# Three copies per block of transposed q and k: VectorE's queue or GpSimd's

## The chip, the cores and the metric

The kernel runs on one core of a Trainium2 chip. A core has five engines that run side by side, each with its own in-order queue of instructions: TensorE (PE, matrix products, with PEld for its weight loads), VectorE (DVE), ScalarE (ACT), GpSimd (POOL) and SyncE (SP, which here does nothing but start DMA transfers). An instruction that has to wait for another engine holds up everything behind it in its own queue. The metric is the device time of one execution in microseconds, as the median of several runs; less is better.

## The reference

One decoder layer over 2048 positions of width 1024. A single projection of the normalised input feeds three token mixers; each is gated, and one output projection adds the result to the input.

```python
def hybrid_layer(x, norm_g, w_in, b_f, q_norm_g, k_norm_g, w_pool, pool_scale, w_out):
    h = rms_norm(x, norm_g)
    proj = jnp.einsum('bsd,de->bse', h, w_in)
    (fq, fk, fv, fg, ff, px, pg, sq, sk, sv, sg) = jnp.split(proj, idx, axis=-1)
    fq = rms_norm(to_heads(fq, FOX_HEADS), q_norm_g)
    fk = rms_norm(to_heads(fk, FOX_HEADS), k_norm_g)
    log_f = jax.nn.log_sigmoid(ff + b_f).transpose(0, 2, 1)
    fox_out = from_heads(forgetting_attention(fq, fk, to_heads(fv, FOX_HEADS), log_f)) * jax.nn.silu(fg)
    pool_out = multiscale_pool(px, w_pool, pool_scale) * jax.nn.silu(pg)
    sb = stick_breaking_attention(to_heads(sq, SB_HEADS), to_heads(sk, SB_HEADS), to_heads(sv, SB_HEADS))
    sb_out = from_heads(sb) * jax.nn.silu(sg)
    mixed = jnp.concatenate([fox_out, pool_out, sb_out], axis=-1)
    return x + jnp.einsum('bse,ed->bsd', mixed, w_out)
```

Forgetting attention ("Fox", 8 heads of 64) is causal softmax attention with a bias from cumulated forget gates. Stick-breaking attention ("Stick", 4 heads of 64) weights position s by sigmoid(z) times the product of one minus sigmoid over the positions between s and t. The pooling branch takes trailing means over 2 to 16 positions.

## The kernel before

The sequence is stored backwards and cut into 16 blocks of 128 positions. The work runs in overlapping stages: Fox over its first four heads (names end in `a`), Fox over the other four (`b`), Stick over its four heads (`s`) with the pooling branch mixed in (`p`), and the output projection (`pr`, `mt`, `xr`). Within a stage the loop runs over blocks, in each block over four heads. Numbers are kept as pairs of float16 (a high and a low part), so most products are made twice or three times.

For each block of `a`, `b` and `s` the function `stacks` (line 454) does the following. ScalarE and VectorE write q and k as float16 pairs into `st` (lines 340 and 341). One DMA transpose, started by SP, turns `st` into `qT`: its first four of eight slots hold k of the four heads, the other four hold q; high parts are in partitions 0 to 63, low parts in 64 to 127. A little later in program order (`later(SCD, ...)`) `place` runs three copies:

```python
        def place():
            pick(KCE, 0).tensor_copy(Kc[j // 4][:, :, o_:o_ + P], qT[:, 0:NH])
            for k in range(2):
                pick(SWE, k).tensor_copy(qT[k * HD:k * HD + HD, 0:NH], qT[HD - k * HD:P - k * HD, NH:2 * NH])
            placed.add(tag)
```

The first (line 466) puts k into the key cache `Ka`, `Kb` or `Ks`, 128 partitions of 512 elements. The other two (line 468) overwrite the place of k in `qT` with q whose high and low halves have changed places, 64 partitions of 512 elements each. `pick` chooses the engine: `v` is VectorE, `g` GpSimd. The products of the scores (line 403, into `spa`, `spb`, `sps`) read both the cache and `qT`, so the first scores of a block wait for all three copies.

What else stands in the queues that matter here. VectorE: in Fox the biased maximum of the scores (`L`, `mm`, line 735), in Stick the running product of the sigmoids (`rrs`, a scan, line 882), in all three the low part of the weights (`pp`, line 432), and the small vectors of the norms and the gates. GpSimd: in Fox the gain on q (`qn`, line 717), the scaling of the block's output (`om`, line 758) and the start of the transfer of the cumulated gates (`cd`, line 562); in Stick a small set to one value (line 877), the causal mask of the sigmoids (a select, line 876, without which the scan can't start) and the copy of the scan's last column (`left`, line 886); at the end the product with the gate (`mt`, line 1033). The weights go through a DMA transpose (`tt<-pp`, line 434) to the product with v (lines 445 and 446, in Stick 902 to 904).

The order in every queue is set before the run by a planner that walks the program and places instructions by its own estimates of time. It is not written out by hand, so a change of one instruction's engine moves others too.

Of the kernel before, what the change touches and what calls it, by code (L numbers as in the profile page):

```python
# [36 lines left out]
GR4 = 0  # L37
GR2 = 1
QSB = 2
SWE = 'vv'  # L40
KCE = 'v'
SCD = 5
M5 = 2
FE = 's'
# [80 lines left out]
def hybrid(ctx: ExitStack, tc, xN, w_in, w_pT, w_out, ng, b_f, qg, kg, w_pool, p_scale, bands, out):  # L125
# [19 lines left out]
    def pick(pattern, k):  # L145
        return {"v": v, "g": g, "s": s}[pattern[k % len(pattern)]]
# [307 lines left out]
    def stacks(tag, j, qsrc, ksrc, sc, Kc):  # L454
# [10 lines left out]
# [5 lines that stand above are left out]
# [842 lines left out]
```

## Time and profile before

| What | Value |
|---|---|
| Median of 3 runs | 1407.43 us (1404.51 to 1409.54) |
| The profiled execution, its own time | 1408.75 us |
| Its span from first to last instruction | 1407.0 us |
| Mean granted TensorE clock | 0.941 of full speed |
| PE busy | 1199.0 us, 85% |
| DVE busy | 1036.6 us, 74% |
| ACT busy | 752.8 us, 54% |
| POOL busy | 182.1 us, 13% |
| DMA queue of SP, share of 16 engines | 80.7% |

Busy time is summed per engine over the span. An engine with a low share can still be the one for which others wait at a given place; the share says only how much room it has on average. The profiled execution is 1.3 us above the median.

### The profile page before, as it was taken

What the parts mean: (1) busy time and instruction counts of PE and PEld (TensorE: products, weight loads), DVE (VectorE), ACT (ScalarE), POOL (GpSimd) and SP (SyncE); (2) the same over time, 40 slices, a digit from 0 to 9 for tenths busy, and PEclk for the clock granted to TensorE, in tenths of its full rate; (3) what the DMA queues carried; (4) which work ended last, traced back from release to release, by engine and by line L of the source; (5) the groups of instructions that cost most, each with busy time, mean ns of one, the idle gap of its engine ahead of it and who ended that gap; (6) DMA issues with size and microseconds to landing.
All of it is one profiled execution on the core that took longest, in us unless ns stands there. A gap on an engine that the chain in (4) does not pass through costs nothing.

```text
span 1407.0 us, 24844 instructions
## 1 busy us (share of the span) xinstructions
PE 1199.0 (85%) x9068; PEld 637.2 (45%) x9068; DVE 1036.6 (74%) x2309; ACT 752.8 (54%) x1430; POOL 182.1 (13%) x327
## 2 busy tenths in 40 slices
PE   7788878786867898989887889889898898889998
PEld 3344444353434454545444444445454454444443
DVE  5787788687967567788788867768687789864741
ACT  6565666665745457556676845455454655431210
POOL 0111010000000001000101022212111113222400
PEclk9899999898989899999999989989999999999999
DMA  6789999999999989988899989786887779999863
GB/s 216 180 186 199 213 220 187 194 217 181 252 180 178 219 210 219 189 171 157 170 219 183 194 199 205 166 178 145 173 169 167 161 178 261 234 253 314 219 178 91
DMA packets 617066, 275.24 MB, mean 196 GB/s; under 512 B 552560, under 2 KB 590832, under 8 KB 616944
## 3 DMA queue, kind: packets, MB, share of 16 engines
q1 hardware_dynamic: 605600, 239.93, 80.7%
q10 hardware_dynamic: 10832, 33.67, 7.6%
q8 instruction: 71, 1.16, 0.3%
q14 instruction: 51, 0.42, 0.1%
q0 software_dynamic: 512, 0.07, 0.0%
HBM read 102.60 MB, written 34.67 MB: 98 GB/s over the span
## 4 chain that ended last, share of the span: by engine, by line
PE 40%; DMA 25%; DVE 15%; issue 9%; ACT 8%; POOL 2%; SPq 1%; ACTq 0%; DVEq 0%; POOLq 0%
PE pr L318 10%; DMA tta<-ppa 6%; DVE rrs L882 5%; DMA ttb<-ppb 5%; PE pqkb L318 4%; PE pvgb L318 4%; DMA xTx<-ppx 3%; PE pqks L318 3%; DMA qTa<-sta 3%; PE pp L318 2%; PE spb L403 2%; PE pqka L318 2%; PE pvgs L318 2%; DMA xTm<-ppm 2%; PE ob L445 2%
## 5 line engine op out<-in xcount | busy, mean ns | idle before, releaser
L318 PE MATMUL pr<-wo,xTm 128*128 128x512 f16 x768 | 171.6, 385 | 6.5 <-DMA xTm<-ppm 5.1
L429 ACT CAST pps<-rrs 128x640 f16<-128x640 f32 (+7 forms) x96 | 76.3, 796 | 129.5 <-DVE rrs L882 113.8
L882 DVE TENSOR_TENSOR_SCAN rrs<-rrs 128x640 f32<-128x640 f32 (+7 forms) x64 | 106.4, 1663 | 27.2 <-POOL rrs L876 18.9
L318 PEld LDWEIGHTS <-xTm 128*128 128x128 f16 x768 | 75.5, 99 | 99.0 <-issue 6.3
L745 ACT ACTIVATE Lb<-Lb,nmb 128x640 f32<-128x640 f32 (+7 forms) x96 | 85.5, 892 | 62.4 <-DVE nmb L739 59.4
L318 PEld LDWEIGHTS <-xTs 128*128 128x128 f16 x768 | 75.1, 100 | 91.3 <-issue 11.5
L318 PEld LDWEIGHTS <-xTb 128*128 128x128 f16 x768 | 75.1, 102 | 89.7 <-issue 15.2
L745 ACT ACTIVATE La<-La,nma 128x640 f32<-128x640 f32 (+7 forms) x96 | 85.4, 890 | 48.7 <-DVE nma L739 42.5
L318 PEld LDWEIGHTS <-xTx 128*128 128x128 f16 x720 | 69.8, 101 | 83.2 <-issue 13.9
L432 DVE TENSOR_TENSOR pps<-rrs,pps 128x640 f16<-128x640 f32 (+7 forms) x96 | 87.3, 919 | 17.0 <-ACT pps L429 15.6
L318 PE MATMUL pp<-auxp,xTp 128*128 128x512 f16 x384 | 96.7, 404 | 2.6 <-DVE vo L341 2.6
L318 PE MATMUL pvgb<-wb,xTb 128*128 128x512 f16 x384 | 97.4, 395 | 1.2 <-DVE omb L779 1.0
L318 PE MATMUL pqkb<-wb,xTb 128*128 128x512 f16 x384 | 97.0, 399 | 1.6 <-DVE oma L779 1.3
L432 DVE TENSOR_TENSOR ppb<-Lb,ppb 128x640 f16<-128x640 f32 (+7 forms) x96 | 88.9, 936 | 11.3 <-ACT ppb L429 10.8
L318 PE MATMUL pqks<-ws,xTs 128*128 128x512 f16 x384 | 95.6, 394 | 0.2 <-DVE vo L341 0.2
L403 PE MATMUL spa<-Ka,qTa 128*128 128x512 f16 (+3 forms) x320 | 79.6, 363 | 18.5 <-DVE mma L735 16.0
L318 PE MATMUL pvgs<-ws,xTs 128*128 128x512 f16 x384 | 92.7, 384 | 1.9 <-DVE ym L1004 1.9
L432 DVE TENSOR_TENSOR ppa<-La,ppa 128x640 f16<-128x640 f32 (+7 forms) x96 | 88.2, 934 | 7.0 <-ACT ppa L429 6.7
L445 PE MATMUL oa<-Va,tta 128*128 128x128 f16 x544 | 61.9, 227 | 36.3 <-DMA tta<-ppa 35.0
L445 PE MATMUL ob<-Vb,ttb 128*128 128x128 f16 x544 | 63.3, 226 | 32.7 <-DMA ttb<-ppb 31.5
L318 PE MATMUL pqka<-wa,xTx 128*128 128x512 f16 x336 | 87.7, 407 | 1.5 <-DVE nma L739 1.5
L874 ACT ACTIVATE rrs<-sps,nc 128x640 f32<-128x640 f32 (+7 forms) x96 | 80.1, 863 | 15.7 <-PE sps L403 15.2
(306 smaller groups left out, 2709.0 us busy)
## 6 DMA issues: line engine op xcount, KB each, us to landing
xn<-in_xN_dram SPq DMA_DIRECT2D x16, 512.0 KB, 6.2
xTd<-xTx ACTq DMA_DIRECT2D x16, 512.0 KB, 4.1
xTb<-xTd ACTq DMA_DIRECT2D x16, 512.0 KB, 4.5
xTs<-xTd ACTq DMA_DIRECT2D x16, 512.0 KB, 4.4
xTp<-xTd ACTq DMA_DIRECT2D x16, 512.0 KB, 4.3
go<-gat SPq DMA_DIRECT2D x16, 512.0 KB, 7.1
mt<-mix SPq DMA_DIRECT2D x16, 512.0 KB, 5.5
xr<-in_xN_dram SPq DMA_DIRECT2D x16, 512.0 KB, 4.1
```

The source lines that it names most:

```text
L318: t.matmul(psum, x[:, xa, kt, :], wt[:, wa, c0:c0 + n], start=(kt == 0 and i == 0), stop=(kt == KT - 1 and i == 2))
L403: t.matmul(sp[:, b - c0 + off:e - c0 + off], qT[:, a * NH + h, :], Kc[b // 512][:, h, b % 512:b % 512 + e - b], start=(a == 0), stop=(a == ...
L429: s.copy(hi, p32)
L432: lo_eng.tensor_tensor(lo, p32, hi, ALU.subtract)
L445: t.matmul(o[:, 0:P], tt[:, b, :], vt, start=first, stop=False)
L745: s.activation(ls[a], ls[a], AF.Exp, bias=nm[:, 0:1], accum_out=la[:, a, h:h + 1])
L874: s.activation(gg, sp, AF.Sigmoid, scale=self.nc2[:, 0:1])
L882: v.tensor_tensor_scan(gg, gg, gg, init, ALU.mult, ALU.bypass)
```

## The change

All three copies of `place`, for all 48 blocks of `a`, `b` and `s`, go into GpSimd's queue. Nothing else is edited.

```diff
-SWE = 'vv'
-KCE = 'v'
+SWE = 'gg'
+KCE = 'g'
```

The planner then makes a new order in all queues. Two places show it. In the rows an operation stands as output<-input with the size of the output; `x2` means two such rows in a row, and the number at a name's end tells one buffer from another.

The first place is in Stick, at the copies of the block whose transposed stack is `qTs_10994`. On VectorE before:

```order
L882 SCALAR_TENSOR_TENSOR rrs_1_0_10976<-rrs_1_0_10976 128x768
L432 TENSOR_TENSOR pps_1_0_10983<-rrs_1_0_10976,pps_1_0_10983 128x768
L466 COPY Ks_10419<-qTs_10994 128x4x128
L468 COPY qTs_10994<-qTs_10994 64x512 x2
L882 SCALAR_TENSOR_TENSOR rrs_2_0_11038<-rrs_2_0_11038 128x768
L909 SCALAR_TENSOR_TENSOR oms_11102<-os_10899,io,oms_11102 128x256
```

On VectorE with the change:

```order
L882 SCALAR_TENSOR_TENSOR rrs_1_0_10976<-rrs_1_0_10976 128x768
L432 TENSOR_TENSOR pps_1_0_10983<-rrs_1_0_10976,pps_1_0_10983 128x768
L909 SCALAR_TENSOR_TENSOR oms_11102<-os_10899,io,oms_11102 128x256
L341 SCALAR_TENSOR_TENSOR vr_11057<-pvgs_10996,vr_11057 128x4x64
L882 SCALAR_TENSOR_TENSOR rrs_2_0_11038<-rrs_2_0_11038 128x768
```

On GpSimd before, the same heads:

```order
L876 AFFINE_SELECT rrs_1_0_10976<-rrs_1_0_10976 128x128
L886 COPY left_10919<-rrs_1_0_10976 128x1
L877 MEMSET rrs_3_0_11111 128x1
L876 AFFINE_SELECT rrs_2_0_11038<-rrs_2_0_11038 128x128
L886 COPY left_10919<-rrs_2_0_11038 128x1
```

On GpSimd with the change:

```order
L876 AFFINE_SELECT rrs_1_0_10976<-rrs_1_0_10976 128x128
L886 COPY left_10919<-rrs_1_0_10976 128x1
L466 COPY Ks_10419<-qTs_10994 128x4x128
L877 MEMSET rrs_3_0_11111 128x1
L468 COPY qTs_10994<-qTs_10994 64x512 x2
L876 AFFINE_SELECT rrs_2_0_11038<-rrs_2_0_11038 128x128
```

The copies have left the stretch of VectorE between two scans, and stand on GpSimd ahead of the select on which the second of these scans (`rrs_2_0_11038`) depends. In 14 of Stick's 16 blocks a select stands within three rows behind the two copies of line 468.

The second place is early in Fox over the first heads, at `qTa_724`, the stack of the third block. On GpSimd with the change:

```order
L758 TENSOR_TENSOR oma_866<-oma_866,rla_968 128x256
L466 COPY Ka_501<-qTa_724 128x4x128
L717 TENSOR_TENSOR qna_936<-qna_936,gain 128x256
L468 COPY qTa_724<-qTa_724 64x512 x2
L466 COPY Ka_501<-qTa_958 128x4x128
```

The cache copy stands behind the scaling of the first block's output (`oma_866`), and the two copies of the halves behind the gain on a later block's q (`qna_936`). Before, none of the three shared a queue with these two products.

## Rows read from the trace of the kernel before

**Rows 1.** The page, busy time by engine: us, share of the span, instructions.

```profile
PE 1199.0 (85%) x9068; PEld 637.2 (45%) x9068; DVE 1036.6 (74%) x2309; ACT 752.8 (54%) x1430; POOL 182.1 (13%) x327
```

**Rows 2.** The page, the chain that ended last: shares of the span.

```profile
PE 40%; DMA 25%; DVE 15%; issue 9%; ACT 8%; POOL 2%; SPq 1%; ACTq 0%; DVEq 0%; POOLq 0%
```

**Rows 3.** Lines 466 and 468: duration ns min/median/max; waits in us, times.

```profile
L466 DVE COPY Ka<-qTa x16: 271/294/296, 52.5 to 405.7; 128x512 f16<-128x512 f16 x16
  DMA qTa<-sta: 25.7, 10
  DMA qTb<-stb: 20.6, 12
  DMA qTs<-sts: 19.7, 9
...
L468 DVE COPY qTa<-qTa x32: 286/289/607, 52.8 to 408.0; 64x512 f16<-64x512 f16 x32
...
  PE sps L403: 13.5, 5
  PE spb L403: 3.3, 3
```

**Rows 4.** The chain in order of time, early in Fox: start us, us, what.

```profile
103.17 6.33 DMA qTa<-sta
...
109.52 0.29 DVE Ka L466
109.81 0.08 DVE w L542
```

**Rows 5.** The same chain, the last such place.

```profile
1010.75 3.26 DMA qTs<-sts
```

**Rows 6.** Windows of 10 us behind 11 such places in Fox: busy us.

```profile
sum 110.00, PE 90.27 PEld 48.87 DVE 100.39 ACT 58.44 POOL 10.62; mean PE 8.21 PEld 4.44 DVE 9.13 ACT 5.31 POOL 0.97
```

**Rows 7.** The same behind three such places in Stick.

```profile
sum 30.00, PE 24.41 PEld 11.90 DVE 27.05 ACT 15.28 POOL 4.65; mean PE 8.14 PEld 3.97 DVE 9.02 ACT 5.09 POOL 1.55
```

**Rows 8.** Groups of GpSimd: out<-in, sizes, count, busy us, mean ns, idle before.

```profile
L805 POOL MEMSET selm<- 128x384 f32 x1 | 0.4, 418 | 4.9 <-DVE ppb L432 4.9
L185 POOL CAST id<-ident 128x128 bf16<-128x128 f32 x1 | 0.3, 296 | 0.0
...
L187 POOL MEMSET zero<- 128x128 bf16 x1 | 0.2, 207 | 0.0
```

**Rows 9.** Line 886 on GpSimd: duration ns min/median/max.

```profile
L886 POOL COPY left<-rrs x64: 185/592/1157, 804.5 to 1240.6; 128x1 f32<-128x1 f32 x64
```

**Rows 10.** Order of time, VectorE near 1186 us: start us, us.

```profile
1185.84 4.45 DVE L882 TENSOR_TENSOR_SCAN rrs<-rrs 128x1024 f32<-128x1024 f32 x1
```

**Rows 11.** The same stretch on GpSimd.

```profile
1185.52 2.61 POOL L1033 TENSOR_TENSOR mt<-mt,go 128x1024 f32<-128x1024 f32 x1 [1.25 <-DMA mix<-ym]
```

**Rows 12.** Groups of VectorE, line 1035: whole span.

```profile
L1035 DVE TENSOR_TENSOR mt<-mt,sg 128x1024 f32<-128x1024 f32 x16 | 24.9, 1558 | 18.1 <-ACT sg L1032 14.3 <-POOL mt L1033 3.8
```

**Rows 13.** The same group from 860 to 1210 us.

```profile
L1035 DVE TENSOR_TENSOR mt<-mt,sg 128x1024 f32<-128x1024 f32 x3 | 3.6, 1200 | 0.0
```

**Rows 14.** Window of the Stick stage: us, then busy (instructions) PE, PEld, DVE, ACT, POOL.

```profile
860.00:1195.00 335.00, 295.37 (x2600) 158.84 (x2598) 260.84 (x313) 177.29 (x268) 60.86 (x148) 0.95 0.81 179
```

**Rows 15.** Waits of 860 to 1210 us: who for whom, us, times, longest.

```profile
DVE rrs L882 <- POOL rrs L876: 16.7, 20, 3.2
```

**Rows 16.** Order of time, VectorE at the copies of `qTs_10994`: start us, us.

```profile
885.56 0.29 DVE L466 COPY Ks<-qTs 128x512 f16<-128x512 f16 x1 [0.28 <-DMA qTs<-sts]
...
886.50 1.76 DVE L882 TENSOR_TENSOR_SCAN rrs<-rrs 128x768 f32<-128x768 f32 x1
```

**Rows 17.** The same on GpSimd: the select of that scan.

```profile
885.16 0.30 POOL L876 TENSOR_SCALAR_AFFINE_SELECT rrs<-rrs 128x128 f32<-128x128 f32 x1 [1.46 <-ACT rrs L874]
```

**Rows 18.** Order of time, VectorE at the cache copy of `qTa_724`.

```profile
76.29 0.28 DVE L466 COPY Ka<-qTa 128x512 f16<-128x512 f16 x1
```

**Rows 19.** GpSimd at the product of `oma_866`.

```profile
80.59 0.61 POOL L758 TENSOR_TENSOR oma<-oma,rla 128x256 f32<-128x256 f32 x1 [0.41 <-DVE oma L779]
```

## The prediction

> **What bounds the kernel now.** I read the busy shares first, then the chain that ended last, then the two lines that move, and last the places where they lie on that chain. The shares [rows 1] show no single bound: PE is at 85%, DVE at 74%, POOL at 13%. The chain [rows 2] agrees: it runs 40% through PE, 25% through DMA transfers and 15% through DVE, so it changes engine all the time, and a gain on DVE is worth only what PE or the transfers can take up behind it.
>
> The moved lines [rows 3] show two things that pull apart. DVE stood idle before the cache copy until the transpose had landed 31 times, for 25.7 + 20.6 + 19.7 = 66.0 us; everything behind the copy in DVE's queue stood too. But PE also waited for the second line: 13.5 us at 5 places in Stick and 3.3 us at 3 places in the second Fox stage. At those 8 places the copies are what PE needs next, and a slower copy is paid at once.
>
> On the chain, the transpose's landing is followed by the copy and then by other work of DVE at 14 places, the first at 103.17 us and the last at 1010.75 us [rows 4, 5]. There the chain goes on through DVE's queue: the wait, not the copy's result, is what costs. In the 10 us behind the copy at the 11 of these places that lie in Fox, DVE is busy 100.39 of 110 us and PE 90.27 [rows 6]; behind the three in Stick DVE has 27.05 of 30 and PE 24.41 [rows 7]. So DVE has a backlog there, and PE has some room behind it.
>
> **The change, part by part.** *What leaves DVE's queue.* 48 cache copies of 0.294 us and 96 copies of halves of 0.289 us [rows 3] are 41.9 us of busy time, and the 66.0 us of waiting leave with them. What this is worth I take in two pieces.
>
> At the 14 places of the chain the gain can't pass PE's idle time behind them: 110 - 90.27 = 19.7 us in Fox and 30 - 24.41 = 5.6 us in Stick. The lower end is 0, if the transfers or ACT hold PE there anyway. I take half of Fox, 9.9 us, because PE's idle time has DMA and DVE behind it alike in the chain (25% and 15%), and nothing of Stick, because there the next scan has to wait for GpSimd all the same (below).
>
> At the other places DVE is only less busy. Part of that comes back, because the two engines hold each other up. A scan of 4.45 us [rows 10] stands beside a GpSimd product of 2.61 us that began 0.3 us before it [rows 11], and the product of line 1035 takes 1.558 us on average over the whole run [rows 12], where GpSimd's own product on the same tile runs close by, against 1.200 us for the three early ones [rows 13]. That is 16 x 0.358 = 5.7 us of DVE for 16 x 2.61 = 41.8 us of GpSimd, or 0.14 us for each microsecond. The copies' 127 us on GpSimd (next part) so give back about 17 us, and 25 us of the 41.9 remain. DVE has 15% of the chain, which makes this worth 3.7 us; ends 0 and, with nothing given back, 6.3 us. The Trainium skill (SBUF — State Buffer, "SBUF: two separate sides") has a rule that speaks against this change: the two engines share one pair of ports, taken whole for an instruction, and a VectorE instruction with two SBUF inputs waits until GpSimd has ended. The row of the 4.45 us scan agrees with it. Taken strictly it would hand back all that DVE saves, and the sum below would come out 3.7 us higher.
>
> *What the three copies take on GpSimd.* No row shows such a copy there. From below: setting 384 elements a partition took 0.418 us and 128 took 0.207 us [rows 8], so 512 without any reading would take 0.52 us, and three 1.57 us. The nearest row that reads is the cast of 128 elements, 0.296 us [rows 8]; the two sets give a fixed part of 0.10 us, which leaves 1.52 ns an element, so 0.88 us for 512, and 2.64 us for the three. (64 partitions count as 128, as they do on DVE.) From above: the copy of line 886, one column wide, takes 0.185 us at best and 0.592 us in the median [rows 9], so up to 0.41 us more each among DVE's work, 3.87 us for three. I take 2.64 us, by the cast, since it too copies from SBUF to SBUF. On DVE the three took 0.87 us, so each block's scores are free 1.77 us later where GpSimd starts as early as DVE did; ends 0.70 and 3.00. Over 48 blocks GpSimd gets 127 us of work and goes from 13% to 22%.
>
> PE pays that at the 8 places where it waits for line 468: 8 x 1.77 = 14.2 us; ends 5.6 and 24.0 us. At the other 40 blocks I take nothing: other products stand ahead of the first scores and cover 1.8 us; if that cover were gone everywhere it would be another 71 us, for which nothing speaks.
>
> *What now stands behind them on GpSimd.* In Fox that is the gain on q, the scaling of the output and the start of the small gate transfer, and at 13% busy they have room. In Stick it is the select, for which scans waited already 20 times, 16.7 us in all [rows 15]. The order shows it at `qTs_10994`: before, the select had run at 885.16 us [rows 17], while DVE waited for the stack and copied from 885.56, and the scan followed at 886.50 [rows 16]. With the change the select comes behind the cache copy, which waits for the same landing, and behind the halves. The wait that DVE loses comes back through the select, 1.77 us longer. DVE can do other work meanwhile, which it mostly has: in the stage it is busy 260.84 of 335 us, idle 22% [rows 14]. So I charge 22% of the three copies at the 14 blocks that have a select close behind: 14 x 2.64 x 0.22 = 8.1 us; ends 0, and 14 x 1.77 = 24.8 us with no other work at hand.
>
> *The sum*, against the profiled execution's 1408.75 us: -9.9 (Fox's waits) - 3.7 (DVE's load) + 14.2 (PE's waits for the copies) + 8.1 (selects) = +8.7, so 1417.4. The profile lies 1.3 us above the median of the runs, so the forecast is 1416 us.
>
> **The rivals.** *DVE's freed queue wins.* The 14 waits vanish, DVE's backlog is gone, and PE takes up all its idle time behind them, in Stick too, because selects run ahead of need. For it: DVE is over 90% busy in just these stretches, and 66.0 us of waiting is more than any one term on the other side. Against it: half of PE's room lies behind transfers, and the select now shares the stack's wait. Price: -25.3 - 3.7 + 14.2 = -14.8, so 1393 us. It decides from the point where PE regains more than 18.6 of the 25.3 us with the selects free, since then the sum is under zero.
>
> *GpSimd's queue holds the copies back.* In the new order some stand behind products that had run later than they. At `qTa_724` the cache copy ran at 76.29 us [rows 18], and the product now ahead of it at 80.59 us [rows 19]: the copies would come 4.9 us later at its end, not 1.8. A few such places in Fox (four would be 19.6 us) on top of the sum give 1436 us. For it: an in-order queue and an order planned on other times than the chip's. Against it: the planner has moved the score products back as well, and most blocks have slack.
>
> *Nothing is left over.* GpSimd copies near the lower end (8 x 0.70 = 5.6 us), the selects cost little, and the first two terms pay for both: -9.9 - 3.7 + 5.6 + 8.1 = +0.1, so 1407.5 us. The Trainium skill (GPSIMD Engine Reference, "Engine selection") leans that way: it calls GpSimd with one input roughly line-rate, which at its 1.2 GHz would be an estimate of 0.43 us for 512 elements. The cast row, 0.296 us for 128 elements, says slower, and no run here shows 512.
>
> That the copies stay on DVE can't be: all 144 stand in GpSimd's order.
>
> **How the numbers follow.** About 0.3% (4.2 us) is what a measurement of this kernel can tell from no change. I give my sum 40%, the freed queue 30%, nothing left over 17%, and the held-back queue 13%. Of my own case a tenth would lie within 0.3%. That makes faster 0.31, the same 0.21, slower 0.48. The lower end of the range takes the freed queue with cheap copies: -25.3 - 3.7 + 5.6 = -23.4, 1384 us; I start at 1386. The upper worst case adds up 24.0 + 24.8 with no gain at all, 1456 us, which needs three bad ends together, so I stop at 1444, beyond the held-back queue. My likeliest case alone would be 1410 to 1428.
>
> **What would show it.** Line 466 and 468 on GpSimd at about 0.88 us each, or 0.5 or 1.3. DVE's busy time down by about 25 us and its idle time before line 466 gone. PE's waits for line 468 at some 31 us, from 16.8. Scans of Stick waiting clearly longer than 16.7 us for GpSimd's selects, and the Stick window longer. I am wrong if the waits for selects don't grow, or if PE's waits for the copies shrink because the planner has put enough other products ahead of the scores; and wrong on the other side if copies in Fox wait several microseconds behind line 758 or 717. The planner's new order of everything else, SP's transposes among them, is a spread in both directions for which I have no row.

## The result and the profile after

The changed kernel takes 1385.47 us in the median of 4 runs (1382.85 to 1393.31), beside 1405.97 us (1398.9 to 1409.54) for the kernel before in 4 runs: a ratio of 0.9861, 95% interval 0.9824 to 0.9898. It is faster by 1.4%, where the forecast was 1416 us. Ratios here and below are worked out from the single runs, without those on record as slow, so they are not quite the quotients of the medians.

The profiled execution has a time of 1382.85 us and a span of 1381.1 us. From its page, busy time by engine and the shares of the chain that ended last, beside [rows 1, 2]:

```profile
PE 1185.5 (86%) x9068; PEld 634.9 (46%) x9068; DVE 1006.6 (73%) x2165; ACT 751.6 (54%) x1429; POOL 304.6 (22%) x471
...
PE 47%; DMA 21%; DVE 11%; issue 9%; ACT 6%; SPq 3%; POOL 2%; ACTq 0%; POOLq 0%; DVEq 0%
```

DVE is 30.0 us less busy and PE 13.5 us, though PE runs the same 9068 products. The chain goes through DVE and transfers less, and through PE more.

The moved lines, beside [rows 3]: duration in ns as min/median/max, and how long the engine stood idle before them.

```profile
L466 POOL COPY Ka<-qTa x16: 609/610/1375, 52.6 to 400.2; 128x512 f16<-128x512 f16 x16
L466 POOL COPY Kb<-qTb x16: 608/610/1548, 423.9 to 733.4; 128x512 f16<-128x512 f16 x16
L466 POOL COPY Ks<-qTs x16: 604/612/1453, 734.9 to 1147.5; 128x512 f16<-128x512 f16 x16
...
  DMA qTb<-stb: 123.1, 15
  DMA qTa<-sta: 106.8, 14
  DMA qTs<-sts: 52.7, 13
...
L468 POOL COPY qTa<-qTa x32: 604/610/1377, 53.3 to 401.6; 64x512 f16<-64x512 f16 x32
...
  PEld L403: 1.8, 1
  PE spa L403: 1.3, 1
```

A copy takes 0.61 us on GpSimd, with 128 partitions or 64, and most of the 144 take just that. GpSimd now waits for the landings, for 282.6 us in all. What stands behind it there is told with Stick, below. Before, two more lines waited for line 468 than [rows 3] show:

```profile
  PEld L403: 20.6, 10
...
  PE spa L403: 0.8, 1
```

So PE's products waited 17.6 us (13.5 + 3.3 + 0.8) and now wait 1.3, and the weight loads waited 20.6 us and now wait 1.8.

Where the time went is read from the stages. Each ends where the next stage's first cache copy starts, and Stick ends at the first row of line 1062. Columns: length, busy (instructions) of PE, PEld, DVE, ACT, POOL, granted clock, DMA share, GB/s. The kernel before, then after; the rows are the two Fox stages and Stick:

```profile
52.50:430.50 378.00, 303.77 (x2338) 164.43 (x2336) 294.56 (x902) 231.32 (x509) 31.86 (x46) 0.92 0.97 201
430.50:764.50 334.00, 280.40 (x2075) 153.02 (x2074) 253.81 (x665) 204.18 (x428) 27.27 (x37) 0.93 0.94 194
764.50:1230.40 465.90, 407.06 (x3539) 221.22 (x3537) 363.08 (x494) 252.72 (x395) 88.60 (x212) 0.95 0.85 186
```

```profile
52.60:423.90 371.30, 299.88 (x2331) 164.67 (x2330) 290.74 (x857) 231.98 (x507) 67.94 (x95) 0.91 0.98 203
423.90:734.90 311.00, 272.76 (x2088) 150.60 (x2087) 242.97 (x613) 203.30 (x430) 58.54 (x83) 0.95 0.99 208
734.90:1200.90 466.00, 405.22 (x3533) 221.00 (x3532) 351.17 (x445) 251.63 (x395) 142.47 (x264) 0.95 0.87 187
```

The second Fox stage is 23.0 us shorter, the first 6.7 us, and Stick in this trace as long as before. What follows Stick is 3.5 us longer (176.6 and 180.1 us). In the two Fox stages PE's idle time falls from 74.2 + 53.6 = 127.8 us to 71.4 + 38.2 = 109.6, by 18.2 us, and its busy time by 3.9 + 7.6 = 11.5 us. In the second stage the transfers fill up as well, from 0.94 to 0.99.

Stick's length hides a trade. Its longest waits of DVE (who for whom, us, times, longest), before and after:

```profile
DVE Ks L466 <- DMA qTs<-sts: 19.7, 9, 4.0
DVE rrs L882 <- POOL rrs L876: 18.6, 24, 3.2
```

```profile
DVE rrs L882 <- POOL rrs L876: 40.2, 28, 4.9
```

The 19.7 us of waiting for the stack have gone, and the scans wait 21.6 us more for the selects, which now stand behind the copies. Timelines of GpSimd and VectorE at one block of Stick show it: the cache copy waits 4.58 us for its landing, the select comes behind it, and the scan waits 4.28 us for the select.

```profile
985.00 0.61 POOL L466 COPY Ks<-qTs 128x512 f16<-128x512 f16 x1 [4.58 <-DMA qTs<-sts]
985.55 0.10 POOL L877 MEMSET rrs<- 128x1 f32 x1
985.60 0.29 POOL L876 TENSOR_SCALAR_AFFINE_SELECT rrs<-rrs 128x128 f32<-128x128 f32 x1
985.95 3.05 POOL L468 COPY qTs<-qTs 64x512 f16<-64x512 f16 x2
...
985.92 2.03 DVE L882 TENSOR_TENSOR_SCAN rrs<-rrs 128x896 f32<-128x896 f32 x1 [4.28 <-POOL rrs L876]
```

### The profile page after: what moved, and what is told of

It reads as the page before. It is cut to its first block, busy times and chain, and to the rows that moved or that the text cites. A ratio compares the mean times of both kernels' runs of the same rounds, so it can differ in the third digit from the quotient of the medians.

```text
span 1381.1 us, 24952 instructions
## 1 busy us (share of the span) xinstructions
PE 1185.5 (86%) x9068; PEld 634.9 (46%) x9068; DVE 1006.6 (73%) x2165; ACT 751.6 (54%) x1429; POOL 304.6 (22%) x471
## 4 chain that ended last, share of the span: by engine, by line
PE 47%; DMA 21%; DVE 11%; issue 9%; ACT 6%; SPq 3%; POOL 2%; ACTq 0%; POOLq 0%; DVEq 0%
PE pr L318 8%; DMA tta<-ppa 5%; DMA ttb<-ppb 5%; PE pqkb L318 4%; PE pvgb L318 4%; PE pqks L318 4%; DMA xTx<-ppx 3%; DVE rrs L882 3%; PE pqka L318 3%; PE pvgs L318 3%; PE pvga L318 3%; PE pp L318 3%; PE spb L403 2%; PE spa L403 2%; PE sps L403 2%
## 5 line engine op out<-in xcount | busy, mean ns | idle before, releaser
L432 DVE TENSOR_TENSOR pps<-rrs,pps 128x640 f16<-128x640 f32 (+7 forms) x96 | 93.5, 988 | 16.4 <-ACT pps L429 16.0
L432 DVE TENSOR_TENSOR ppb<-Lb,ppb 128x640 f16<-128x640 f32 (+7 forms) x96 | 87.8, 927 | 11.3 <-ACT ppb L429 11.2
L318 PE MATMUL pvgb<-wb,xTb 128*128 128x512 f16 x384 | 93.4, 386 | 0.0
L445 PE MATMUL ob<-Vb,ttb 128*128 128x128 f16 x544 | 61.4, 224 | 28.7 <-DMA ttb<-ppb 28.2
```

What stands on the lines that cost most here:

```text
L318: t.matmul(psum, x[:, xa, kt, :], wt[:, wa, c0:c0 + n], start=(kt == 0 and i == 0), stop=(kt == KT - 1 and i == 2))
L432: lo_eng.tensor_tensor(lo, p32, hi, ALU.subtract)
L445: t.matmul(o[:, 0:P], tt[:, b, :], vt, start=first, stop=False)
```

## The experiments

Three theories stood against each other. By the first, VectorE's wait for the landing, in order, is what cost time in Fox, and its end is the gain. By the second (the theory of VectorE's pace), a Fox stage lasts as long as VectorE is busy plus some fixed idle time, so any load taken off VectorE comes back, whatever it is. By the third, the new order that the planner writes for all queues is the cause, and the copies are not.

All ratios are to the kernel before, run on the same chip. In the tables "a", "b" and "Stick" are the lengths of the three stages in the profiled execution, with the ends named above.

**Which stage pays.** Line 466 and 468 take their engine from the stage. The first kernel has GpSimd in Fox and VectorE in Stick, the second the reverse (`"s"` for `"ab"`):

```diff
-            pick(KCE, 0).tensor_copy(Kc[j // 4][:, :, o_:o_ + P], qT[:, 0:NH])
+            eng = g if tag[0] in "ab" else v
+            eng.tensor_copy(Kc[j // 4][:, :, o_:o_ + P], qT[:, 0:NH])
...
-                pick(SWE, k).tensor_copy(qT[k * HD:k * HD + HD, 0:NH], qT[HD - k * HD:P - k * HD, NH:2 * NH])
+                eng.tensor_copy(qT[k * HD:k * HD + HD, 0:NH], qT[HD - k * HD:P - k * HD, NH:2 * NH])
```

> The copies of the two Fox stages on GpSimd, those of Stick on VectorE as before. By the comparison of the two traces the time was won between the first copies of the second Fox stage and the first copies of Stick (334 us before, 311 after), a little in the first Fox stage, and none in Stick. Theory 'wait': the same gain as with all copies moved, 1383 to 1390 us, and scans wait for selects as in the kernel before (about 17 us). If Stick's part had in truth helped as well (its lost wait made up for by later selects), 1392 to 1400 us. Rival 'order': anything from 1385 to 1406 us.

> The copies of Stick on GpSimd, those of both Fox stages on VectorE as before. Theory 'wait' with selects that give it back: no change within 0.5%, 1400 to 1410 us, and scans waiting for selects twice as long as before (some 30 us against 17). If moving them helps by itself: 1390 to 1398 us. By the prediction's own term for the selects it would be slower by about 8 us, 1412 to 1416 us.

Measured: Fox alone 1382.86 us, 0.9879 [0.9833, 0.9925]; Stick alone 1397.36 us, 0.996 [0.9924, 0.9996]. Fox alone has, within the intervals, as much of a gain as the whole change; the copies of Stick alone are worth 0.4% (by the interval nothing to 0.8%). The trade in Stick shows in the traces of both: the scans wait 34.5 us for the selects with Stick's copies moved alone, and 18.8 us with Fox's alone.

**What of VectorE's relief pays.** Three kernels add something back to VectorE in the kernel after: its load without a wait for a landing (four small copies a block out of `st`, some 42 us in all), its wait without the load (a copy of two columns out of the landed `qT`, in `place`), and twice the load.

```diff
+        v.tensor_copy(fill, st[:, 0, 0:2])
+        v.tensor_copy(fill, st[:, 0, 2:4])
+        for k in range(2):
+            v.tensor_copy(fill[k * HD:k * HD + HD], st[HD - k * HD:P - k * HD, 1, 0:2])
```

```diff
+            v.tensor_copy(seen, qT[:, NH, 0:2])
```

> All three copies stay on GpSimd; VectorE gets four extra copies a block (128x256 and 64x256 float16, about 0.2 us each, some 40 us in all), made right after the stack is written, so that they wait for no transfer. They write into a scratch tile and nothing reads it. Theory 'wait' (what helped is that VectorE's queue no longer stands before a transfer that hasn't landed): the load alone takes back little, 1385 to 1392 us, a ratio of 0.985 to 0.990 to the kernel before. Rival 'load' (what helped is 42 us less work on VectorE): 1400 to 1408 us, ratio 0.995 to 1.002. Rival 'order' (the planner happened on a better order of everything else): any value between, and PE's waits elsewhere than behind the copies.

> All three copies stay on GpSimd; VectorE gets one copy of two columns a block (about 0.06 to 0.15 us, some 5 us in all) that reads the part of the transposed stack which no copy overwrites, and so waits for the same landing as the copies did before. Theory 'wait': VectorE stands idle before it for some 40 to 66 us and most of the gain is gone, 1398 to 1408 us, ratio 0.995 to 1.002. Rival 'load': the gain stays, 1385 to 1390 us. Rival 'order': 1385 to 1405 us, without a match between the idle time and the time lost.

> All copies on GpSimd, and twice the extra VectorE load of the first run (eight copies a block of 0.22 us, 56 us in the two Fox stages, waiting for no transfer; scratch, read by nothing). Theory 'pace': the Fox stages grow by those 56 us over the changed kernel's 682, to 735 to 742 us, and the whole kernel to 1425 to 1445 us. Rival 'order': no growth in step with the load, 1395 to 1415 us, as with the single load. Rival 'PE sets the pace and has room': below 1410 us.

Measured: the load 1402.48 us, 1.0014 [0.9982, 1.0046]; the wait 1410.98 us, 1.0088 [1.0057, 1.0119]; twice the load 1405.12 us, 1.002 [0.9987, 1.0052]. The second portion of load, another 42 us of VectorE's time, moves the ratio from 1.0014 to 1.002, within the intervals. So an amount of load can hardly be what the first portion cost. To see whether any added instruction does it, a fourth kernel has one copy of two columns out of `st` after its transpose is started, with no wait for a landing and 8 us in all:

```diff
+        v.tensor_copy(seen, st[:, 1, 0, 0:2])
```

> All copies on GpSimd; VectorE gets one copy of two columns a block from the stack before its transpose, so the same small instruction as in the second run, but waiting for no transfer (48 x 0.17 = 8 us, of which 5.5 us in the two Fox stages). Theory 'pace' (in Fox VectorE sets the pace: a stage lasts as long as its busy time, its waits for the transposed stack and an idle rest of about 80 us in the first and 68 us in the second Fox stage): Fox 682 + 5.5 = 688 us, whole kernel 1388 to 1394 us. Rival 'order' (any change of the planner's order loses what the changed kernel won by chance): 1398 to 1412 us, as in the two runs that put something back.

Measured: 1404.9 us, 1.0022 [0.9983, 1.006]. It has neither load nor wait, and yet the gain is gone. My theory of VectorE's pace fell here, as it had with twice the load, for which it expected 1425 us or more. Such an edit also makes the planner write a new order for every queue, so part of what these kernels lose may be order. The trace of this one has a loss elsewhere. PE's waits in the first Fox stage (50 to 425 us), after and then with the tiny copy:

```profile
PE pf L327 <- DMA xTx<-ppx: 19.0, 6, 8.8
```

```profile
PE pf L327 <- DMA xTx<-ppx: 30.2, 7, 8.9
```

PE waits 11.2 us longer for the transposed inputs (30.0 us in all in a repeat, below), and in the second stage VectorE waits for PE's scores. VectorE's waits there, after and with the tiny copy:

```profile
DVE Lb L735 <- PE spb L403: 14.8, 14, 2.8
```

```profile
DVE Lb L739 <- PE spb L403: 28.4, 22, 3.9
DVE Lb L739 <- PE spb L405: 13.5, 5, 5.5
```

The profile of the kernel with the wait shows what was meant: the wait is back. VectorE's idle time before the added copy, and the kernel's two Fox stages in windows:

```profile
L471 DVE COPY seen<-qTb x16: 171/172/519, 436.6 to 766.0; 128x2 f16<-128x2 f16 x16
...
  DMA qTb<-stb: 31.0, 12
  DMA qTs<-sts: 28.9, 11
  DMA qTa<-sta: 21.7, 10
```

```profile
53.70:436.60 382.90, 309.49 (x2323) 168.47 (x2322) 296.59 (x874) 234.42 (x513) 67.02 (x95) 0.87 0.94 198
436.60:771.70 335.10, 284.25 (x2140) 155.55 (x2139) 251.74 (x631) 203.08 (x425) 65.10 (x85) 0.93 0.93 194
```

The second stage is at 335.1 us again, with the transfers at 0.93 and the clock at 0.93, much as before the change. In the tiny copy's trace, where VectorE waits for no landing, the clock of that stage is 0.93 too (0.95 in a repeat, below), and the transfers are at 1.00.

**How much is order.** Three pairs with the copies on VectorE and on GpSimd, each pair with one number changed that sets the planner's order: `LEADS[3]` from 11 to 12, `LEADS[1]` from 10 to 12 (both are places of a table that the planner adds to its due times), and `SCD`, how much later in program order `place` runs, from 5 to 9.

```diff
-LEADS = {0: 21, 1: 10, 2: 10, 3: 11,
+LEADS = {0: 21, 1: 10, 2: 10, 3: 12,
...
```

```diff
-SCD = 5
+SCD = 9
```

> The kernel before, with one number of the table that paces projections against scores changed by one (block 3 of the first Fox stage, 11 to 12): the planner's order changes in some 15% of PE's rows, the engines of all work stay. Theory 'pace': as the kernel before within 0.5%, 1397 to 1412 us. Rival 'order': anything from 1380 to 1420 us.

> The changed kernel with the same number changed as in the run beside it. Theory 'pace': as the changed kernel within 0.5%, 1380 to 1393 us, and 1.0% to 1.8% under the run beside it. Rival 'order': no fixed distance between the two; the gain may be gone, 1400 us and more.

> The kernel before (copies on VectorE), with the copies placed nine ticks after the stack instead of five. If VectorE's waits for the stack are what the change removed, a later place should remove them too without GpSimd: waits before line 466 well under 66 us, and by the size of the changed kernel's gain 1385 to 1395 us. If the distance between the changed kernel and the one before is mostly the planner's order, anything from 1385 to 1415 us, without step to those waits.

> The changed kernel with the copies placed nine ticks after the stack. Theory 'small gain of the move plus order' (the move itself is worth some 0.5%, the rest of the 1.4% is the order that the planner happened on): 0.2% to 1% under the run beside it. Theory 'move' (the whole gain is the move): 1.1% to 1.8% under it, unless the waits have gone there as well. Theory 'order alone': either side of it.

> The kernel before with another number of the pacing table changed (block 1 of the first Fox stage, 10 to 12), so a third order of the planner with all copies on VectorE. By the two orders measured so far, 1397 to 1412 us; under 'order alone' 1380 to 1420 us.

> The changed kernel with that same number, so a third order with all copies on GpSimd. Theory 'small gain of the move plus order': 1385 to 1405 us, 0.2% to 1% under the run beside it. Theory 'move': 1380 to 1392 us. Theory 'order alone': 1380 to 1415 us, either side of the run beside it.

| Pair | Copies on VectorE | On GpSimd |
|---|---|---|
| as given | 1 | 0.9861 [0.9824, 0.9898] |
| `LEADS[3]` 12 | 1.0026 [0.9999, 1.0054] | 0.996 [0.9927, 0.9992] |
| `LEADS[1]` 12 | 0.9964 [0.993, 0.9998] | 0.9871 [0.9799, 0.9943] |
| `SCD` 9 | 1.0058 [1.002, 1.0096] | 0.9823 [0.9763, 0.9883] |

GpSimd is ahead in each pair, by 0.7 to 2.4 points, and one number moves VectorE's kernels over 0.9 points (0.9964 to 1.0058) and GpSimd's over 1.0 (0.9861 to 0.996). So the move gains in more than one order, and how much is partly the luck of the order. The two kernels of each changed number ran side by side on one chip, so the 0.7 points are not a difference between chips.

Two things speak against the wait as the only cost. The expectation for `SCD` 9 on VectorE was that a later place takes the waits away; they grew instead, from 66.0 to 77.9 us (28.7 + 29.0 + 20.2), so this run is no test of their removal. And the time does not follow the length of the waits: VectorE waits for the stack in Fox for 46.3, 50.2, 63.2 and 57.7 us in the four kernels of the left column, from the top, and the one with the longest waits is the fastest.

**Repeats that were meant as more.** I then put the wait, the load, the tiny copy and the Fox-only split into the kernel with `SCD` 9, taking it for another order. Set beside each other row by row, buffer numbers left out, the orders of 5 and 9 are the same in every queue as soon as the copies stand on GpSimd; only with the copies on VectorE do they differ. So the run of `SCD` 9 on GpSimd is a repeat of the kernel after, and the next four repeat earlier ones. The expectations below speak of a second order that there was not.

> The copies on GpSimd placed nine steps later in the program (the 1380 us kernel), plus a two-column copy on VectorE that reads the landed stack, so that VectorE waits for the transpose again. By the theory that VectorE's waits are the cost it loses most of the 2.3% between this pair: 1400 to 1415 us. By the theory that VectorE's load is the cost it stays at 1380 to 1388 us (48 small copies are about 8 us of VectorE at a few tenths of the chain). By the theory that the planner's order alone decides, it lies anywhere from 1380 to 1410 us, and the two runs beside it do too, in no order of their own.

> The same 1380 us kernel, plus the three copies' load on VectorE (four copies of the same size, about 42 us in all, from the stack before its transpose, so that nothing waits for a landing). By the load theory 1400 to 1412 us; by the wait theory 1380 to 1390 us; by the order theory anywhere from 1380 to 1410 us.

> The same 1380 us kernel, plus a two-column copy on VectorE from the stack before its transpose: neither the load (8 us in all) nor the wait for a landing. By the wait theory and by the load theory alike 1380 to 1388 us. If it loses more than 10 us, as the same edit did with the copies five steps later, what is lost comes with any new VectorE instruction at this place of the program, through the planner's order.

> The copies of the two Fox stages on GpSimd and those of Stick on VectorE, all placed nine steps later. If the gain lies in Fox alone, and Stick is a little better with its copies on VectorE, 1376 to 1384 us. If Stick's copies on GpSimd gain in this order, 1385 to 1400 us.

Measured: the wait 1410.22 us, 1.0049 [1.0028, 1.0071]; the load 1397.38 us, 0.9957 [0.9927, 0.9986]; the tiny copy 1406.18 us, 1.0029 [1.0001, 1.0058]; Fox alone 1384.57 us, 0.988 [0.9844, 0.9916]. As repeats they confirm the first round, but can't free the comparison from the order. They also show how far two batches of one program lie apart: 0.4 points for the kernel after (0.9861 and 0.9823) and for the wait (1.0088 and 1.0049), 0.6 for the load (1.0014 and 0.9957). Within this batch the tiny copy costs more than the five times longer load, and the wait 4 us more than the tiny copy.

The last two were to put a VectorE copy without a wait at the place of the one with the wait:

```diff
+            v.tensor_copy(seen, id16[:, 0:2])
```

> The kernel after, plus a two-column copy on VectorE at the very place where the earlier experiment let VectorE wait for the landed stack (1411 us), but this one reads a constant, so it waits for nothing. By the theory that VectorE's wait is the cost: 1382 to 1394 us, and the second Fox stage at 311 to 322 us. By the theory that any VectorE instruction added in this place of the program loses the gain through a new order: 1402 to 1412 us, like the one with the wait.

> The same copy of a constant on VectorE, in the kernel with the copies placed nine steps later on GpSimd (1380 us; with the wait 1410 us). By the wait theory 1378 to 1392 us; by the theory of the added instruction 1400 to 1412 us.

Measured: 1379.51 us, 0.985 [0.9812, 0.9888], and 1378.41 us, 0.9827 [0.9795, 0.9859]. The trace shows what became of the copies:

```profile
L471 DVE CAST seen<-id x48: 159/172/173, 2.5 to 24.2; 128x2 f16<-128x2 bf16 x48
```

With nothing to wait for, all 48 were put into the first 25 us of the program, and every queue's order behind them is that of the kernel after. So these two are the change once more, and no test of an added instruction in the midst of the queue. What they give is a neighbour for the kernel with the wait: by the names and sizes of what a row writes and reads, 15485 of PE's 17886 rows stand at the same position in both, the closest of the add-back kernels to the change (13681 for the load, 13356 for the tiny copy; 12744 for the kernel before). That is no proof that order plays no part: `LEADS[3]` 12 on GpSimd is as close, with 15603, has no wait, and loses 1.0 of the change's 1.4 points. Windows of the first of the two, the Fox stages:

```profile
54.00:425.80 371.80, 301.92 (x2331) 165.80 (x2330) 289.61 (x855) 232.01 (x507) 65.71 (x94) 0.91 0.98 203
425.80:736.80 311.00, 269.07 (x2089) 149.23 (x2088) 241.66 (x613) 203.74 (x430) 60.53 (x83) 0.96 1.00 208
```

With the wait in the queue the stages take 11.1 and 24.1 us more. Of the 24.1 us some 7 are a matter of where the stage is cut: PE runs 51 more products in it (2140 and 2089), at 0.13 us each.

**All orders side by side.** Stage lengths by whether VectorE waits for the landing of the stack in Fox, two numbers where an order was run twice:

| Kernel | VectorE waits in Fox | a, us | b, us |
|---|---|---|---|
| before | yes | 378.1 | 333.9 |
| `LEADS[3]` 12, VectorE | yes | 377.0 | 333.7 |
| `LEADS[1]` 12, VectorE | yes | 368.4 | 334.4 |
| `SCD` 9, VectorE | yes | 373.5 | 340.0 |
| after, wait put back | yes | 382.9; 379.4 | 335.1; 340.8 |
| after (and `SCD` 9) | no | 371.2; 369.1 | 311.1; 311.7 |
| `LEADS[1]` 12, GpSimd | no | 375.2 | 315.7 |
| `LEADS[3]` 12, GpSimd | no | 381.1 | 323.7 |
| after, load put back | no | 382.2; 375.9 | 328.8; 321.8 |
| after, load twice | no | 379.3 | 326.5 |
| after, tiny copy | no | 390.5; 386.5 | 339.0; 329.3 |

In the second stage the five orders with the wait take 334 to 341 us, and those without it 311 to 329, with one reading of the tiny copy (339) as the exception; that profiled execution took 1416.96 us, 12 above the median of its runs, and the one of the load with 321.8 us took 1389.02, 8 below. In the first stage there is no such gap. (The Fox-only and Stick-only kernels aren't listed: in Fox their orders are all but those of the kernel after and the kernel before. Their second stages take 310.9 and 319.6 us, and 332.1.)

The gap is narrower than it looks, because the second stage doesn't hold the same work in each order. PE runs 2140 and 2162 products in it with the wait put back and 2153 and 2156 with the tiny copy, beside 2088 after. Taken to 2088 products at PE's mean time for one in each stage, an estimate from these windows, the wait put back has 328 and 331 us, the tiny copy 330 and 320, the load 327 and 321, twice the load 325, and the four kernels with the copies on VectorE 333 to 339. The added copies without a wait then cost much of what the wait costs, and two traces of one order lie up to 10 us apart.

The third stage, Stick, is a little shorter with its copies on GpSimd: 453 to 466 us in the seven traces that have them there and nothing added in the midst of VectorE's queue, and 463 to 470 in the six with them on VectorE. The trace of the kernel after, with its 466.0 us, is the longest of the seven.

## Why the prediction was wrong

*What leaves DVE's queue* is the step that failed. I put -9.9 us on Fox's waits, and the Fox stages are 29.7 us shorter. Two things were wrong in it.

First the half. I let the gain be no more than PE's idle time in 10 us behind the 11 Fox places that lie on the chain [rows 6], 19.7 us, and took half of it. PE's idle time in Fox fell by 18.2 us, nearly the whole bound. DVE waited at 22 places in Fox, for 46.3 us [rows 3]; whether the gain came from the 11 places that I had counted or from the others too, no run here tells.

Then a part that the sum did not have at all. PE's busy time in Fox fell by 11.5 us for 4413 and 4419 products. In the second stage, where 7.6 us of it lie, a product takes 130.6 ns instead of 135.1, and the granted clock is 0.95 instead of 0.93 of its upper level of 2.4 GHz (the lower is 1.2), after PE's busy share rose from 84% to 88%. The clock's part is some 2% of 280 us, an estimate of 5 to 6 us from these rows; in the first stage the clock did not rise (0.92 and 0.91). That a busier PE brought the higher clock is not shown: in the first stage PE is 81% busy both after the change and with the wait put back, at 0.91 and 0.87.

*DVE's load*, -3.7 us: its busy time fell by 30.0 us, where I said 25 (11.9 of the 41.9 came back, not 17). What that is worth alone was not settled. The second 42 us of load moved the ratio by under 0.1 points, which speaks for a small term; the first 42 us came with 17 and 12 us in two runs, beside the 1385.5 us of the kernel after, and a tiny copy at the same place with about 20, so the larger part of that isn't the amount of load.

*PE's waits for the copies*, +14.2 us, had the wrong sign. I had read 16.8 us of waits where there were 17.6 for PE's products and another 20.6 for its weight loads. The copies came out cheaper than my 0.88 us, but the waits fell to 1.3 and 1.8 us for another reason: in the new order the scores come later behind the copies, as the text on what would show me wrong had it. In Stick a score started within 0.3 us of a block's last copy in 8 of the 16 blocks before, and in 2 after. I had priced the places of the old order, and there was a new one. The Trainium skill (GPSIMD Engine Reference, "Engine selection") calls one input roughly line-rate, and my estimate from it was 0.43 us; the trace has 0.61, beside 0.294 us on VectorE [rows 3]. That estimate had no fixed part, and the one by the cast was too high.

*Selects in Stick*, +8.1 us: the mechanism was right, the price was not. Scans wait 21.6 us more for the selects, nearly what the lost waits for the stack gave back (19.7 us), and Stick is 466 us as before in this trace, and by the traces of all orders a few microseconds shorter. The kernel with Stick's copies left on VectorE is, within the intervals, as fast as the change. It is a trade of one wait for another that costs nothing.

Of the rivals, *DVE's freed queue wins* (1393 us) came true in Fox, though not as it was written: the selects of Stick don't run ahead of need. It is still too slow by 7.5 us, because it carried the +14.2 of PE's waits. Its point of decision was also wrong: 18.6 us still charges the selects with 8.1; with them free it is 10.5 us. The result lies half a microsecond below the range.

**What is shown and what is not.** That the move gains is shown by four pairs (three orders on GpSimd, one of them run twice and more), and that most of it lies in Fox by the split by stage. That VectorE's in-order wait for the landing is what costs there is argued and not shown. For it: put back, the wait takes all of the gain and more, twice; the transfers and the clock of the second stage go back with it; and the four kernels with the copies on VectorE have the longest second stages once the products are made equal. Against it stands the tiny copy, which lost nearly as much without a wait (1405 and 1406 us, beside 1411 and 1410). Against it also stand that the kernel with the longest waits is the fastest of the four on VectorE, and that an order without the wait, as close to the change's as that of the wait put back, loses most of the gain. In the tiny copy's trace PE waits longer for the transposed inputs; an order that does this also stands behind the slow GpSimd kernel of `LEADS[3]` (32.2 us of that wait, and 381.1 us in the first stage). That fits a loss by order, but why a reader of `st` brings it is open. How much of the 29.7 us in Fox is the wait and how much the new order stays open. To run both engines' kernels in one fixed order, which would settle it, was not tried.

## What to carry to other kernels

When an instruction that waits for a transfer leaves a busy in-order queue for one that has nothing to do, don't halve what the engine behind it can regain without a row that says so, and leave room for its busy time: here Fox became 29.7 us shorter, 18.2 of PE's idle time and 11.5 of its busy time. Price the waits behind a moved instruction in the new order if that can be read, since a planner may have covered them. And before a variant is taken for an independent trial, compare the orders row by row: two settings of one number gave the same program, and an added instruction without a wait ran in the head of the program. Where a planner writes the order, an edit that adds an instruction changes it too: 8 us of small copies without a wait lost the whole gain here. Such an edit can't single out a cause unless the order is held.

## What the runs showed of the hardware that was not expected

A float16 copy of 512 elements a partition on GpSimd takes 0.610 us with 64 partitions and with 128. 101 of the 144 copies stay under 0.65 us and 28 take over 1 us, up to 2.4. At each of these 28 a product of line 432 or a scan of line 882 was running on VectorE when the copy began, or began within 0.03 us of it, and the copy ended 0.40 to 0.48 us after one of these. In the timelines shown with Stick, the two copies that begin at 985.95 us beside a scan of 2.03 us take 3.05 us instead of 1.22. So for the most part it was GpSimd that waited: its copies took 115.4 us, 27.6 more than 144 times 0.61. VectorE paid little for this: its products of line 432 in the Fox stages and its scans of line 882 kept their mean durations within 3%. Groups after, of line, engine and tile: busy us, mean ns, idle before.

```profile
L882 DVE TENSOR_TENSOR_SCAN rrs<-rrs 128x640 f32<-128x640 f32 (+7 forms) x64 | 104.3, 1636 | 50.3 <-POOL rrs L876 42.3 <-POOL rrs L877 7.4
L432 DVE TENSOR_TENSOR pps<-rrs,pps 128x640 f16<-128x640 f32 (+7 forms) x96 | 93.5, 988 | 16.4 <-ACT pps L429 16.0
L432 DVE TENSOR_TENSOR ppa<-La,ppa 128x640 f16<-128x640 f32 (+7 forms) x96 | 89.8, 954 | 5.5 <-ACT ppa L429 5.4
L432 DVE TENSOR_TENSOR ppb<-Lb,ppb 128x640 f16<-128x640 f32 (+7 forms) x96 | 87.8, 927 | 11.3 <-ACT ppb L429 11.2
```

Before, these means were 1663, 919, 934 and 936 ns: only the products in Stick became clearly longer, by 69 ns each or 6.6 us in all. The rule of the Trainium skill that was cited against the change (SBUF — State Buffer, "SBUF: two separate sides") says that whichever of the two instructions starts first keeps the shared ports to its end while the other is blocked. The long copies agree with it, with GpSimd as the one that is blocked; the prediction gave only the half in which VectorE waits, and so took it for a loss of all that VectorE saves. Of the 41.9 us of copies 30.0 stayed saved.
